# Neighbourhood attention's scores as two strided 512-column products per head, with zero-padded low parts

## The chip, the cores and the metric

One core of a Trainium2 chip runs the whole program in one launch. The metric is the time of one execution in device microseconds; a kernel's time is the median of several executions.

## What is computed

Two layers of a hybrid block work on 512 latent tokens (a grid of 8 rows by 64 columns) and 256 context tokens of width 1024. Each layer has four mixers of four heads with 64 features (neighbourhood attention, a gated linear recurrence, retention, differential attention), an output projection and a gated feed-forward. The change touches neighbourhood attention alone. For a query at grid row r and column c the keys are a window of 8 rows by 16 columns, with a relative position bias, and all 256 context tokens, under one softmax:

```python
s_win = (jnp.einsum('bqhd,brqjhd->bhqrj', qr, kw).astype(jnp.float32)
         + bias[None].astype(jnp.float32))
s_ctx = jnp.einsum('bqhd,bchd->bhqc', qr, k_ctx).astype(jnp.float32)
s = jnp.concatenate([s_win.reshape(b, h, GRID_W, n_win), s_ctx], axis=-1)
p = jax.nn.softmax(s, axis=-1).astype(v.dtype)
```

In the first layer the context's own queries also attend to the context.

## The kernel before, in words

All matrix products keep nearly full fp32 accuracy: each operand is split into a high part and the rest, its low part, and a product is made of the parts' products. For the scores the split lies along the contraction. A head has 64 features, and TensorE contracts over 128 rows, so `qk_stacks` (line 1161) builds for each head a key operand whose rows are [high; low] and a query operand whose rows are [high; high] (`stack_k`, line 985, and `stack_q`, line 996). One product over 128 rows then gives high times high plus high times low. A second product over 64 rows adds the low part of Q times the high part of K: the low parts of both heads share one tile `ql`, head 0 in rows 0 to 63 and head 1 in rows 64 to 127.

`na_unit` (line 1204) handles 128 queries of a pair of heads. Latent tokens stand in an order that makes a unit's 256 window keys a contiguous range that starts at `WBASE[j]`; the 256 context keys lie in another tile (`Kc`). So a head takes four products of 256 columns, two over 128 rows and two over 64:

```python
for ko, kk in ((0, st["K"][h][:, k]), (256, st["Kc"][h])):
    mm(o[:, ko:ko + 256], lhsT=st["Q"][h][:, q], rhs=kk, start=True, stop=False)
    mm(o[:, ko:ko + 256], lhsT=st["ql"][r, q], rhs=kk[r], start=False, stop=True)
```

VectorE then adds bias and mask and takes the maximum, ScalarE takes the exponential (`softmax_rows`, line 1244), the probabilities are turned on TensorE, copied, and multiplied with V. There are 2 layers x 2 head pairs x 4 query tiles = 16 units with 4 such pairs of products each, so 64 pairs, and `na_ctx` (line 1255) has 2 head pairs x 2 query tiles x 2 heads = 8 more, in the first layer alone. `steps_na` (line 1937) gives the units out one at a time.

The order of the instructions is not that of the code. The program is recorded, and a planner (class `Issue`, `run` at line 346) issues every instruction itself, engine by engine, from a list schedule with costs of its own: the first one of the program whose operands and places are there. Its price of a product depends on the columns alone. A string `ORDER` sets in which turn the mixers' steps enter the program, so that projections and other mixers stand between the units. Tiles are places of a few kinds: 26 of 1024 columns (T), 6 of 512 (t), 7 of 3072 (D), and in PSUM two double banks (s) and four single ones (a). The profile puts every instruction on line 535, where the planner issues it, so they are told apart by tile names and shapes: score products are `s<-T,T`.

Of the kernel before, what the change touches and what calls it, by code (L numbers as in the profile page):

```python
# [11 lines left out]
F32 = mybir.dt.float32  # L12
F32R = mybir.dt.float32r
# [73 lines left out]
class View:  # L87
    """a view of a buffer whose place is chosen later; ap: the same view of the buffer's first place"""
# [36 lines left out]
class Tag:  # L125
    """equal places for buffers"""
# [10 lines left out]
    def place(self, slot, dt):  # L137
        """of SBUF a new tile on the place, as a tile's elements keep one type"""
# [8 lines left out]
class Kind:  # L147
    """a limit on how many places buffers of a kind may hold at once, for each phase of the program"""
# [23 lines left out]
class Issue:  # L172
    """the engines' interface of a Bass: keeps the instructions, and issues them in the order of a list schedule: the
    first one of the program whose operands and places are there"""
# [25 lines left out]
    def box(self, ap, row):  # L200
        """partitions and columns (or DRAM elements) that a view touches"""
# [8 lines left out]
    def any(self, *alts):  # L210
        """one instruction that any of several engines can carry out: (engine, function, operands, options)"""
        self.add(*alts[0], alts=alts)

    @contextmanager
    def together(self):
        """TensorE's instructions that go out one right after the other"""
        self.calls = []
        yield
        calls, self.calls = self.calls, None
        self.add("tensor", "group", calls, {})  # L220
# [64 lines left out]
    def port(self, op):  # L285
        """whether it takes the SBUF port that DVE and GpSimd share: 2: its write side too"""
# [54 lines left out]
    def larger(self, b, spare, front):  # L341
        """whether a buffer can have one of the larger places"""
# [3 lines left out]
    def run(self):  # L346
# [21 lines left out]
        # a PSUM buffer is not taken before what its readers take besides it is under way  # L368
# [18 lines left out]
        def held(op, eng):  # L387
            """until when the other engine holds the port that op takes"""
# [4 lines left out]
        def start(op, now, eng):  # L393
            """the earliest time of op from now on, or None while a place has to be kept for others"""
# [22 lines left out]
        while len(order) < N:  # L417
# [50 lines left out]
            # semaphores to wait for beyond the one an instruction can carry  # L468
# [69 lines left out]
class Net:  # L538
# [35 lines left out]
    def mark(self):  # L574
        """a phase of the program begins"""
# [8 lines left out]
    def accs(self, n):  # L584
        """n times [128, 1024] in PSUM, by halves"""
# [40 lines left out]
    # ---------------------------------------------------------------- set-up  # L626
# [44 lines left out]
    def setup2(self):  # L671
# [5 lines left out]
        # softplus(y) for y = -ret_decay (broadcast), -lru_lambda (per channel)  # L677
# [28 lines left out]
        # lambda of the differential attention  # L706
# [17 lines left out]
        # relative position bias, spread over the query's column: E2[c, (l h u), X] = rpb[u, X - 1 - c]  # L724
# [13 lines left out]
    # ------------------------------------------------------------ modulation  # L738
    def mod_quarter(self, l, va, vb, q):
        """quarter q of the two vectors of a norm's shift and scale, as columns"""  # L740
# [42 lines left out]
    def mod(self, l, pairs):  # L783
        """two vectors of the modulation at a time: columns for a norm's shift and scale, or gates in DRAM"""
# [40 lines left out]
    def mod_gain(self, dst, src, o, n):  # L825
        """g_pre * (1 + scale) from columns of the scale"""
# [3 lines left out]
    def gate_rows(self, l, which, n):  # L830
        """gate * g_post on all partitions, for the latents and the context"""
# [7 lines left out]
    # ------------------------------------------------------------------ norm  # L839
    def rstd(self, ms, n):  # L840
        """(ms + eps) ** -0.5 of n columns"""
# [27 lines left out]
    def hT_alloc(self):  # L869
        """8 feature chunks of 512 latents and 256 context tokens, 4 to a tile: high and low parts"""  # L870
# [7 lines left out]
    def to_hT(self, xs, hT, part, sc, sh, pairs=range(4)):  # L878
        """xs: normed token tiles of a part -> modulated, feature-major, split"""
# [20 lines left out]
    def half_hT(self, t, late):  # L900
        """half of all token tiles, normed -> the second block's input: modulated, feature-major, split"""
# [1151 lines left out]
```

## Time and profile before

| what | value |
|---|---|
| runs | 1779.1, 1770.55, 1769.05 us (median 1770.55) |
| the profiled execution's span | 1774.8 us |
| the profiled execution's own time | 1779.1 us, the only run that is longer than the span: 4.3 us lie around it |
| PE busy | 1678.9 us (95%) |
| VectorE, ScalarE, GpSimd busy | 1251.0, 832.7, 187.9 us (70%, 47%, 11%) |
| DMA | 143 GB/s on average |

PE is TensorE's matmul side, PEld its weight loads, DVE VectorE, ACT ScalarE, POOL GpSimd. In a timeline row the first number is the start from the span's begin, the second the modelled duration. A matmul's duration contains the way through the array, so what a product costs the stream is read from one start to the next. The form `64*128 64x256` is a product over 64 rows with 128 output rows and 256 columns; `128*128 128x256` contracts over 128 rows. PEclk 1.00 is the full TensorE clock (2.4 GHz), 0.50 its lower level (1.2 GHz).

### The profile page before, as it was taken

Reading aid. Unit: us, or ns where it says so; the run is one execution under the profiler, and the core shown is the slowest. Engines: PE = TensorE matmul, PEld = TensorE weight load, DVE = VectorE, ACT = ScalarE, POOL = GpSimd, SP = SyncE. Lnnn points to the kernel's source line nnn. Section 1 sums busy time; section 2 is a strip of 40 time slices with the busy share of each in tenths; the row PEclk is TensorE's granted clock in tenths of the full one; section 3 lists DMA queues with packets and bytes.
Section 4 is the critical chain, followed back from the end, with each engine's and each line's share of the span. In section 5 each row is a group of like instructions: output and inputs, shape, how many; then the busy total and the mean of one; then the engine's idle time right before and its main releaser. Section 6 shows DMA issues by size and latency. Waiting matters only on the chain. (4 is left out here: it accounts for less than half of the span.)

```text
span 1774.8 us, 27125 instructions
## 1 busy us (share of the span) xinstructions
PE 1678.9 (95%) x10575; PEld 1446.7 (82%) x10575; DVE 1251.0 (70%) x2108; ACT 832.7 (47%) x1385; POOL 187.9 (11%) x181
## 2 busy tenths in 40 slices
PE   4899799799999999999999979999999999999997
PEld 2788677557786999999987858888877899999886
DVE  3476764654668988788679998886865688777442
ACT  3357742565656343333344466755544453343221
POOL 1010102000101101110000050132101100112000
PEclk9999999889999999999999999999997999999999
DMA  8661458744647242423665645444224443333332
GB/s 260 194 149 42 128 194 222 221 167 158 235 167 253 74 131 66 129 76 110 243 215 179 223 168 158 101 113 105 60 79 159 133 112 96 108 96 95 107 121 81
DMA packets 210456, 254.17 MB, mean 143 GB/s; under 512 B 13524, under 2 KB 163504, under 8 KB 210328
## 3 DMA queue, kind: packets, MB, share of 16 engines
q1 hardware_dynamic: 205392, 240.80, 42.8%
q0 software_dynamic: 4608, 11.54, 3.6%
q8 instruction: 83, 1.36, 0.3%
q14 instruction: 45, 0.37, 0.1%
q10 hardware_dynamic: 328, 0.11, 0.0%
HBM read 223.95 MB, written 28.69 MB: 142 GB/s over the span
## 5 line engine op out<-in xcount | busy, mean ns | idle before, releaser
L535 ACT ACT_TABLE_LOAD x41 | 52.6, 1283 | 13.0 <-PE s L535 6.9
L535 PE MATMUL s<-D_4u,D_5u 128*128 128x512 f32 (+1 forms) x66 | 18.1, 358 | 7.8 <-DVE T_3u L535 5.1
L535 PE MATMUL a<-D_0u,T_17u 128*128 128x256 f32 (+2 forms) x72 | 21.6, 331 | 0.0
L535 PE MATMUL s<-D_6u,D_4u 128*128 128x256 f32 (+1 forms) x33 | 9.9, 386 | 12.0 <-DMA D_4u<-dstk 10.7
L535 DVE TENSOR_TENSOR st_3u<-st_3u 128x1 f32<-128x1 f32 x2 | 0.3, 160 | 29.7 <-ACT T_13u L535 23.7
L535 PEld LDWEIGHTS s<-D_4u,D_5u 128*128 128x128 f32 x66 | 10.8, 190 | 11.7 <-DVE T_3u L535 5.3
L535 POOL TENSOR_TENSOR st_6u<-st_3u,mhalf_0u 128x1 f32<-128x1 f32 (+1 forms) x4 | 4.4, 1104 | 149.4 <-DVE st_3u L535 149.4
L535 ACT COPY t_3u<-s 128x384 f32<-128x384 f32 (+1 forms) x16 | 6.8, 426 | 28.5 <-PE s L535 27.9
L535 POOL DMA_DIRECT2D D_4u<-dstk x16 | 9.4, 589 | 96.1 <-DMA dstk<-T_17u 78.2
L535 PEld LDWEIGHTS s<-D_6u,D_4u 128*128 128x128 f32 x33 | 5.9, 204 | 16.5 <-issue 11.6
L535 PE MATMUL a<-D_0u,T_3u 128*128 128x256 f32 (+2 forms) x56 | 18.2, 336 | 0.0
L535 ACT ACTIVATE t_4u<-t_4u 128x384 f32<-128x384 f32 (+1 forms) x13 | 6.2, 476 | 23.6 <-DVE t_4u L535 23.6
L535 PE MATMUL a<-D_0u,T_4u 128*128 128x384 f32 (+2 forms) x60 | 16.2, 326 | 0.7 <-ACT T_1u L535 0.7
L535 PE MATMUL a<-D_0u,T_19u 128*128 128x384 f32 (+2 forms) x56 | 16.3, 339 | 0.0
L535 PE MATMUL a<-D_2u,T_1u 128*128 128x512 f32 (+1 forms) x40 | 15.2, 379 | 0.0
L535 PE MATMUL a<-D_2u,T_17u 128*128 128x512 f32 (+1 forms) x44 | 15.1, 343 | 0.0
L535 ACT COPY t_0u<-s 128x384 f32<-128x384 f32 (+1 forms) x13 | 5.8, 446 | 19.6 <-PE s L535 19.1
L535 ACT ACTIVATE t_0u<-t_0u 128x384 f32<-128x384 f32 (+1 forms) x12 | 5.9, 489 | 18.6 <-DVE t_0u L535 18.6
L535 ACT ACTIVATE T_13u<-s 128x512 f32<-128x512 f32 x4 | 2.4, 594 | 26.0 <-PE s L535 26.0
L535 PE MATMUL a<-D_3u,T_1u 128*128 128x512 f32 (+2 forms) x36 | 14.2, 394 | 0.0
L535 PE MATMUL a<-D_2u,T_3u 128*128 128x512 f32 (+1 forms) x40 | 14.1, 354 | 0.0
L535 PEld LDWEIGHTS a<-D_0u,T_17u 128*128 128x128 f32 x72 | 13.1, 190 | 1.2 <-ACT T_17u L535 0.3
(4181 smaller groups left out, 6816.8 us busy)
## 6 DMA issues: line engine op xcount, KB each, us to landing
D_4u<-dstk POOLq DMA_DIRECT2D x16, 384.0 KB, 6.9
T_6u<-in_w_mod_dram SPq DMA_DIRECT2D x8, 512.0 KB
T_20u<-in_w_mod_dram SPq DMA_DIRECT2D x7, 512.0 KB
T_4u<-in_w_mod_dram SPq DMA_DIRECT2D x7, 512.0 KB
T_21u<-in_w_in_dram SPq DMA_DIRECT2D x7, 512.0 KB
T_23u<-in_w_mod_dram SPq DMA_DIRECT2D x6, 512.0 KB
T_16u<-in_w_mod_dram SPq DMA_DIRECT2D x6, 512.0 KB
T_13u<-in_w_mod_dram SPq DMA_DIRECT2D x6, 512.0 KB
```

Source lines behind the costliest of these rows:

```text
L535: getattr(getattr(self.real, op.eng), fn)(*map(real, a), **{x: real(v) for x, v in k.items()})
```

## The change

Keys of latents and of the context now lie in one tile for each head (columns 0 to 511 and 512 to 767; the context's queries take columns 768 to 1023), so that the window and the context are two runs of 256 columns at a fixed stride, and one product reads both as its 512 columns. Each head gets its own tile half for Q's low parts, with zeros in the other 64 rows, so that the second product too contracts over all 128 rows (the rows of K's low parts meet the zeros). GpSimd writes the zeros. The context's low parts (`qlc`) are in a tile of kind t. The diff also drops comments, which is left out here.

```diff
     def stack_q(self, dst, lo, src, h, scale=None):
...
         self.scale(dst[o], src[r], s)
+        nc.gpsimd.memset(lo[o].bitcast(F32), 0.0)
         nc.vector.scalar_tensor_tensor(lo[r], src[r], s, dst[r].bitcast(F32), ALU.mult, ALU.subtract)
...
     def qk_stacks(self, l, hT, b, sq, sk, ctx):
-        K, Q = self.T(F32R, "K"), self.T(F32R, "Q")
-        KQc, ql = self.T(F32R, "KQc"), self.T(F32R, "ql")
-        st = dict(K=[K[:, 0:512], K[:, 512:1024]], Q=[Q[:, 0:512], Q[:, 512:1024]],
-                  Kc=[KQc[:, 0:256], KQc[:, 256:512]], Qc=[KQc[:, 512:768], KQc[:, 768:1024]],
-                  ql=ql[:, 0:512], qlc=ql[:, 512:768])
+        halves = lambda t: [t[:, 0:t.shape[1] // 2], t[:, t.shape[1] // 2:]]
+        ks = [self.T(F32R, "K") for _ in range(2)]
         ps, pc = self.proj(l, self.w_blk(l, sk, b), hT, True)
         for h in range(2):
-            self.stack_k(st["K"][h], ps, h)
-            self.stack_k(st["Kc"][h], pc, h)
+            self.stack_k(ks[h][:, 0:512], ps, h)
+            self.stack_k(ks[h][:, 512:768], pc, h)
         yield
+        st = dict(K=ks, Q=halves(self.T(F32R, "Q")), ql=halves(self.T(F32R, "ql")))
         ps, pc = self.proj(l, self.w_blk(l, sq, b), hT, ctx)
+        if ctx:
+            st.update(Qc=[t[:, 768:1024] for t in ks], qlc=halves(self.nc.buf("t", F32R)))
...
     def na_unit(self, l, b, st, vt, vmix, tab, out, j):
...
-                r = slice(64 * h, 64 * h + 64)
-                o = sps[:, h * 512:h * 512 + 512]
-                for ko, kk in ((0, st["K"][h][:, k]), (256, st["Kc"][h])):
-                    mm(o[:, ko:ko + 256], lhsT=st["Q"][h][:, q], rhs=kk, start=True, stop=False)
-                    mm(o[:, ko:ko + 256], lhsT=st["ql"][r, q], rhs=kk[r], start=False, stop=True)
+                o = sps[:, h * 512:h * 512 + 512].rearrange("p (a n) -> p a n", a=2)
+
+                kk = st["K"][h][:, w:1024 - w].rearrange("p (a n) -> p a n", a=2)[:, :, 0:256]
+                mm(o, lhsT=st["Q"][h][:, q], rhs=kk, start=True, stop=False)
+                mm(o, lhsT=st["ql"][h][:, q], rhs=kk, start=False, stop=True)
...
     def na_ctx(self, b, st, vt, out, j):
...
-                K = st["Kc"][h]
+                K = st["K"][h][:, 512:768]
                 o = sps[:, h * 512:h * 512 + 256]
                 mm(o, lhsT=st["Qc"][h][:, q], rhs=K, start=True, stop=False)
-                mm(o, lhsT=st["qlc"][r, q], rhs=K[r], start=False, stop=True)
+                mm(o, lhsT=st["qlc"][h][:, q], rhs=K, start=False, stop=True)
```

TensorE's order at the second unit of the first layer. T_15 holds the latents' stacked keys, T_13 those of the context, T_22 and T_12 the queries' high and low parts, so a row with 128x256 here is a score product; rows with ident are transposes for differential attention. Before:

```order
L535 MATMUL s_81<-ident_0u_102,T_5u_3299 128x128 x6
L535 MATMUL s_80<-T_15u_2993,T_22u_3289 128x256
L535 MATMUL s_80<-T_15u_2993,T_12u_3224 128x256
L535 MATMUL s_80<-T_13u_2924,T_22u_3289 128x256
L535 MATMUL s_80<-T_13u_2924,T_12u_3224 128x256
L535 MATMUL s_80<-T_15u_2993,T_22u_3289 128x256
L535 MATMUL s_80<-T_15u_2993,T_12u_3224 128x256
L535 MATMUL s_80<-T_13u_2924,T_22u_3289 128x256
L535 MATMUL s_80<-T_13u_2924,T_12u_3224 128x256
L535 MATMUL a_79<-ident_0u_102,T_6u_3353 128x128 x2
```

With the change (T_13 and T_16 are the two heads' keys, T_24 and T_3 the queries' high and low parts, the last row is a product with V in differential attention):

```order
L535 MATMUL s_81<-ident_0u_102,T_19u_3292 128x128 x6
L535 MATMUL s_80<-T_13u_2930,T_24u_3281 128x512
L535 MATMUL s_80<-T_13u_2930,T_3u_3110 128x512
L535 MATMUL s_80<-T_16u_2940,T_24u_3281 128x512
L535 MATMUL s_80<-T_16u_2940,T_3u_3110 128x512
L535 MATMUL a_78<-T_20u_3355,T_18u_865 64x128
```

The unit's eight products have become four; its neighbours are the same kinds of work. TensorE's order is unchanged up to the stretch with the first layer's units, and again from the end of the first layer's output projection to the second layer's mixers, and after these to the end. In the two stretches with units, score products, transposes, projections and the first products of the output projection change places by some rows.

GpSimd's order at the start of the program, with the change (T_7 and T_8 belong to another step, t_0 and t_1 hold the low parts of the context's queries; "x2" is both heads):

```order
L535 MEMSET T_7u_131 128x256
L535 MEMSET T_8u_133 128x256
L535 MEMSET t_0u_135 64x256 x2
L535 MEMSET t_1u_141 64x256 x2
L535 ISA
L535 TENSOR_TENSOR st_1u_228<-st_0u_213,mhalf_0u_104 128x1
```

The two rows with 64x256 are new; all others were there in this order. GpSimd's order in the first layer's mixers, with the change (T_3 and T_17 hold Q's low parts of the two head pairs, the DMA belongs to differential attention, the TENSOR_TENSOR rows are roots for norms):

```order
L535 MEMSET T_9u_2776 128x256
L535 DMA D_4u_2795<-dstk 32x4x768 x4
L535 MEMSET T_3u_3110 64x512 x2
L535 MEMSET T_17u_3573 64x512 x2
L535 TENSOR_TENSOR st_19u_3785<-st_18u_3780,mhalf_0u_104 128x12
L535 TENSOR_TENSOR st_5u_4400<-st_3u_4384,mhalf_0u_104 128x1
```

The rows with 64x512 are new, and two subtractions of 128x1024 that stood between the last two rows are gone from here: VectorE has them now. The memsets wait for nothing but a place, so the planner puts them ahead of the tiles' first use, those of the context at the very start of the program.

## Rows read from the trace of the kernel before

**Rows 1.** The page: span, busy time of the engines, granted clock in 40 slices.
```profile
span 1774.8 us, 27125 instructions
...
PE 1678.9 (95%) x10575; PEld 1446.7 (82%) x10575; DVE 1251.0 (70%) x2108; ACT 832.7 (47%) x1385; POOL 187.9 (11%) x181
...
PEclk9999999889999999999999999999997999999999
```

**Rows 2.** Timeline of PE at the first unit (start us, us, engine, line, operation, shapes, count).
```profile
367.02 0.39 PE L535 MATMUL s<-T_15u,T_22u 128*128 128x256 f32 x1
367.34 0.38 PE L535 MATMUL s<-T_15u,T_12u 64*128 64x256 f32 x1
367.65 0.38 PE L535 MATMUL s<-T_13u,T_22u 128*128 128x256 f32 x1
367.96 0.38 PE L535 MATMUL s<-T_13u,T_12u 64*128 64x256 f32 x1
```

**Rows 3.** Timeline of PE: full products that follow each other, 512 and 256 columns.
```profile
429.21 0.28 PE L535 MATMUL a<-D_1u,T_10u 128*128 128x256 f32 x1
429.33 0.28 PE L535 MATMUL a<-D_0u,T_0u 128*128 128x256 f32 x1
...
1318.36 0.40 PE L535 MATMUL a<-D_2u,T_17u 128*128 128x512 f32 x1
1318.60 0.40 PE L535 MATMUL a<-D_0u,T_17u 128*128 128x512 f32 x1
```

**Rows 4.** Timeline of PE at the half clock: units' products, then two full ones of 512 columns.
```profile
383.53 0.58 PE L535 MATMUL s<-T_15u,T_12u 64*128 64x256 f32 x1
...
384.55 0.58 PE L535 MATMUL s<-T_13u,T_12u 64*128 64x256 f32 x1
...
1342.08 0.63 PE L535 MATMUL a<-D_1u,T_1u 128*128 128x512 f32 x1
1342.51 0.63 PE L535 MATMUL a<-D_3u,T_20u 128*128 128x512 f32 x1
...
1348.48 0.58 PE L535 MATMUL s<-T_9u,T_10u 64*128 64x256 f32 x1
```

**Rows 5.** Busy time by stretch: us, busy us (instructions) by engine, PEclk, DMA share, GB/s.
```profile
core 0: us, PE busy (x) PEld busy (x) DVE busy (x) ACT busy (x) POOL busy (x), PEclk, DMA share, GB/s
366.00:381.00 15.00, 15.00 (x104) 9.26 (x106) 10.72 (x32) 9.76 (x25) 0.00 (x0) 1.00 0.48 172
381.00:392.00 11.00, 11.00 (x52) 5.91 (x46) 2.74 (x12) 4.75 (x11) 0.00 (x0) 0.54 0.71 242
...
428.00:446.00 18.00, 18.00 (x88) 12.17 (x80) 8.99 (x28) 7.98 (x18) 0.00 (x0) 1.00 0.49 165
...
1278.00:1300.00 22.00, 22.00 (x137) 15.97 (x136) 10.82 (x30) 10.76 (x23) 2.55 (x2) 1.00 0.08 25
...
1323.00:1330.00 7.00, 6.72 (x39) 5.05 (x39) 3.89 (x9) 1.56 (x2) 1.64 (x1) 0.51 0.25 75
1330.00:1333.00 3.00, 3.00 (x15) 1.93 (x13) 2.15 (x4) 2.50 (x3) 0.00 (x0) 1.00 0.80 169
1333.00:1350.00 17.00, 17.00 (x43) 11.72 (x44) 5.13 (x19) 5.20 (x11) 4.23 (x3) 0.51 0.44 157
```

**Rows 6.** Timeline of PE: the wait ahead of a unit in the second layer.
```profile
1323.28 0.58 PE L535 MATMUL s<-T_13u,T_10u 64*128 64x256 f32 x1 [2.34 <-DVE T_10u L535]
```

**Rows 7.** Timeline of POOL's memsets and of DVE beside them, and a DVE operation without.
```profile
1174.64 0.61 DVE L535 TENSOR_SCALAR T_18u<-T_18u,st_28u 128x768 f32<-128x768 f32 x1
...
1214.48 0.30 POOL L535 MEMSET T_23u<- 128x256 f32 x1
...
1215.24 0.30 POOL L535 MEMSET T_21u<- 128x256 f32 x1
...
1214.55 1.28 DVE L535 COPY T_9u<-st_7u 128x512 f32<-128x512 f32 x1 [0.54 <-POOL st_7u L535]
```

**Rows 8.** Groups of POOL's instructions: the widest memset (busy us, mean ns).
```profile
L535 POOL MEMSET T_14u<- 128x1024 f32 x1 | 1.0, 958 | 0.0
```

More of the change, by code (lines that the diff above doesn't have):

```diff
@@ L1161, in qk_stacks @@
     def qk_stacks(self, l, hT, b, sq, sk, ctx):
-        K, Q = self.T(F32R, "K"), self.T(F32R, "Q")
-        KQc, ql = self.T(F32R, "KQc"), self.T(F32R, "ql")
-        st = dict(K=[K[:, 0:512], K[:, 512:1024]], Q=[Q[:, 0:512], Q[:, 512:1024]],
-                  Kc=[KQc[:, 0:256], KQc[:, 256:512]], Qc=[KQc[:, 512:768], KQc[:, 768:1024]],
-                  ql=ql[:, 0:512], qlc=ql[:, 512:768])
+        halves = lambda t: [t[:, 0:t.shape[1] // 2], t[:, t.shape[1] // 2:]]
+        ks = [self.T(F32R, "K") for _ in range(2)]
         ps, pc = self.proj(l, self.w_blk(l, sk, b), hT, True)
         for h in range(2):
-            self.stack_k(st["K"][h], ps, h)
-            self.stack_k(st["Kc"][h], pc, h)
+            self.stack_k(ks[h][:, 0:512], ps, h)
+            self.stack_k(ks[h][:, 512:768], pc, h)
         yield
+        st = dict(K=ks, Q=halves(self.T(F32R, "Q")), ql=halves(self.T(F32R, "ql")))
         ps, pc = self.proj(l, self.w_blk(l, sq, b), hT, ctx)
+        if ctx:
+            st.update(Qc=[t[:, 768:1024] for t in ks], qlc=halves(self.nc.buf("t", F32R)))
         for h in range(2):
-            self.stack_q(st["Q"][h], st["ql"], ps, h, 0.125)
+            self.stack_q(st["Q"][h], st["ql"][h], ps, h, 0.125)
             if ctx:
-                self.stack_q(st["Qc"][h], st["qlc"], pc, h, 0.125)
+                self.stack_q(st["Qc"][h], st["qlc"][h], pc, h, 0.125)
         return st
@@ L1208, in na_unit @@
             q = slice(j * 128, j * 128 + 128)
-            k = slice(WBASE[j], WBASE[j] + 256)
+            w = WBASE[j]
             whole = lambda a: [(a, 128, 0)]
@@ L1262, in na_ctx @@
             for h in range(2):
-                r = slice(64 * h, 64 * h + 64)
-                K = st["Kc"][h]
+                K = st["K"][h][:, 512:768]
                 o = sps[:, h * 512:h * 512 + 256]
                 mm(o, lhsT=st["Qc"][h][:, q], rhs=K, start=True, stop=False)
-                mm(o, lhsT=st["qlc"][r, q], rhs=K[r], start=False, stop=True)
+                mm(o, lhsT=st["qlc"][h][:, q], rhs=K, start=False, stop=True)
             nc.vector.reduce_max(neg, sps.rearrange("p (h n) -> p h n", h=2)[:, :, 0:256], axis=AX.X, negate=True)
```

## The prediction, made before the changed kernel ran

> **What bounds the kernel now.** I read the page first, then the timeline of TensorE around the score products, then busy time by stretch. The page [rows 1] shows PE busy for 1678.9 of 1774.8 us, 95%, with DVE at 70% and the rest at half or less, and the full clock in nearly every slice. So time taken out of TensorE's stream is worth up to its full amount, if the others keep up. A busy PE need not stream, though, and the timeline shows where it does not. In a unit [rows 2] products over 128 and over 64 rows alternate, and each starts 0.31 to 0.32 us after the one before: 0.62 us from one 64-row product to the next (367.34 to 367.96). Full products that follow each other [rows 3] are 0.12 us apart at 256 columns and 0.24 us at 512. The columns of a pair are worth 0.24 us; the other 0.38 us go with the two changes between 128 and 64 rows. Nothing is waited for there: no row of rows 2 shows idle time. At the half clock [rows 4] a pair takes 1.02 us (383.53 to 384.55) and a full product of 512 columns 0.43 us (1342.08 to 1342.51).
>
> In the stretches with units PE has no gaps but one: 15.00 of 15.00 us, 18.00 of 18.00, 22.00 of 22.00 [rows 5], and one wait of 2.34 us for VectorE's write of Q's low part [rows 6]. So the gain falls on the path.
>
> **The change part by part.**
>
> *Products.* There are 64 pairs in the units and 8 in the context's attention (from the loops). Of the 64, 13 run at the half clock: 2 at 383.53 and 384.55, 3 from 1323.28, and 8 up to 1348.48 [rows 4, 6]. A pair of 256 columns, a full and a 64-row product, becomes half of a pair of 512-column products, that is one product of 512 columns in place of each pair. The new products read their columns in two runs, which no row before shows. Lower bound: 0.24 us, contiguous 512 columns [rows 3]. Upper bound: 0.62 us, if the second run were to cost as much as a change of rows [rows 2]. I take 0.24, as both runs are read by one instruction with one set of weights, and two separate 256-column products already follow each other at 2 x 0.12 [rows 3].
> - 51 pairs at the full clock: 51 x (0.62 - 0.24) = 19.4 us.
> - 13 at the half clock: 13 x (1.02 - 0.43) = 7.7 us.
> - 8 of the context: 8 x (0.62 - 2 x 0.12) = 3.0 us.
>
> Sum: 30.1 us less on PE. The zeros add no columns. Sixty-four weight loads go as well; PEld overlaps PE and is below it in every stretch [rows 5], so I count nothing for them.
>
> *Memsets.* Twelve, eight of 64x512 and four of 64x256. A memset of 256 columns takes 0.30 us [rows 7], of 1024 columns 0.96 us [rows 8], so 512 columns are about 0.52 (estimate between the two): 8 x 0.52 + 4 x 0.30 = 5.4 us on POOL, which is 11% busy. Their cover is POOL's idle time: the order puts them ahead of the tiles' first use. But they can hold DVE: a copy of 128x512 beside four memsets took 1.28 us, while a longer operation of 128x768 takes 0.61 without one [rows 7]. The Trainium skill, "SBUF — State Buffer", section "SBUF: two separate sides", says that GpSimd and some VectorE operations take turns on a shared pair of ports, and whoever comes second is blocked for the whole of the other's instruction; that speaks against writing zeros on GpSimd, the row agrees, and by it alone the twelve could cost VectorE up to 5.4 us. By the row, the context's memsets lie at the start of the program, and the eight others hold DVE for at most 4.2 us. DVE is not the path in those stretches (10.72 of 15.00 us, 8.99 of 18.00) [rows 5], so I take 1 us on the end, between 0 and 4.2.
>
> *Order.* Two weight subtractions move from POOL to DVE, and score products shift by some rows. At the changed places this is of either sign; bounds are the one wait seen in these stretches, 2.3 us [rows 6], either way per layer. I take 0.
>
> *Places.* The context's low parts hold two of six t places from the start; Q's low parts hold a T place earlier than before. The order of PE, DVE and ACT in the first stretches stays as it was, so nothing there lacks a place by the plan. Cost 0; the upper bound is once more a wait like 2.3 us [rows 6].
>
> *What is late next.* Where units follow each other closely the other engines get less time. From 366 to 381 there are 12 pairs, 12 x 0.38 = 4.6 us, which leaves 10.4 us for DVE's 10.72 and ACT's 9.76 [rows 5]. There DVE becomes the bound, and with work that cannot be packed fully I count 2 us lost. From 428 to 446 (18 pairs, 6.8 us, 11.2 left for 8.99 and 7.98) and from 1278 to 1300 (16 pairs, 6.1 us, 15.9 left for 10.82 and 10.76) they fit, but each unit's softmax sits between its scores and its transposes; 2 us for both. From 1323 to 1350 DVE and ACT are light; the 2.34 us wait stays, since the second product still needs Q's low part.
>
> Sum: 30.1 - 1 - 2 - 2 = 25 us. The profiled execution took 1779.1 us and would take 1754; it is 8.5 us above the median of the runs shown, so for the median I forecast 1770.55 - 25 = 1745.5 us.
>
> **The rivals.** Half a per cent, 9 us, is about what a measurement can tell from no change.
>
> *Softmax takes over.* VectorE and ScalarE set the pace in the stretches with units, and PE waits. For it: the stretch from 366 has no room left (above). Against: in the others DVE and ACT are at half [rows 5]. If half of the 30 us goes into waits and the memsets and subtractions cost what they can, 30 / 2 - 5 = 10 us remain: 1760.
>
> *The clock recovers.* PEclk is near a half from 381 to 392 and in two of the three stretches from 1323 to 1350 [rows 5]: about 10, 7 and 17 us, 34 in all. Less the 7.7 us already taken out, 26 us run at the half clock, which would take 13 at the full one. For it: what goes are products that leave the array without a stream for 0.38 of 0.62 us. Against: transposes and narrow products around them stay. It gives 25 + 13 = 38 us: 1732.
>
> *The clock falls for longer (slower).* Shorter products bring PE to its next wait sooner. The half clock from 1323 came right with the 2.34 us wait [rows 5, 6]. If in the stretches from 366 to 462 and 1278 to 1350 the lower clock held for longer, every microsecond of streaming done there would take two. It decides from 25 us of further work at the half clock; above 34 the kernel is slower by more than 9 us. With 45 us: 1770.5 - 25 + 45 = 1790. Against: the new products stream without a break, and PE has no idle time in nearly all of these stretches.
>
> *It does not do what it says.* If the two runs of a strided product cost 0.62 us, the upper bound, the units gain nothing and the context's 3 us are spent on memsets: 1770.
>
> **How the numbers follow.** The forecast, most of the 30 us reaching the end: 0.70, with 1735 to 1756 for its own range (all of 30 plus 5 from order; or 15). Softmax takes over: 0.13. Clock recovers: 0.10. Clock falls: 0.04. No effect: 0.03. Range: 1731 to 1760, which takes in the forecast, the recovered clock and the better half of the softmax case. Faster by over 0.5%: 0.70 + 0.10 + 0.10 of the softmax case = 0.90. Within: 0.03 + 0.03 = 0.06. Slower: 0.04.
>
> **What would show it.** In the profile after there should be no row of form 64*128 64x256 and 64 new ones of 128x512 on s; their starts 0.24 us apart at the full clock (0.62 would be the strided cost, and wrong); 64 fewer matmuls than 10575; PE's busy time down by 25 to 30 us, with its idle time up by less than 6. The stretch that was 366 to 381 should be bounded by DVE. If PE's busy time falls by 30 and the span by less than 15, the second theory is right; a longer half clock in PEclk would be the fourth. The forecast is wrong if the new products' spacing is not near 0.24, or if PE waits for DVE or ACT for more than 10 us in these stretches.

## The result, and the profile after

The changed kernel takes 1743.83 us (median of four executions, 1742.3 to 1750.7), the kernel before 1769.8 us beside it (median of four): a ratio of 0.985, 95% interval 0.981 to 0.989. That is 26 us less; 1745.5 us was forecast. A second set of six executions gives 1744.1 us and 0.987 (0.984 to 0.991).

The page of the changed kernel, answering to [rows 1] (its own execution took 1743.3 us):

```profile
span 1741.2 us, 27012 instructions
...
PE 1642.4 (94%) x10511; PEld 1425.6 (82%) x10511; DVE 1247.9 (72%) x2108; ACT 830.4 (48%) x1385; POOL 190.9 (11%) x193
...
PEclk9999899899999999999999989999999999999999
```

There are 64 matmuls and 36.5 us of PE's busy time less; DVE and ACT do what they did. PE's idle time, the span less busy, went from 95.9 to 98.8 us. The span fell by 33.6 us, more than the medians did; why is seen below.

The timeline of PE at a unit of the first layer, between products of projections, answers to [rows 2]:

```profile
422.56 0.40 PE L535 MATMUL a<-D_0u,T_0u 128*128 128x512 f32 x1
422.80 0.39 PE L535 MATMUL s<-T_1u,T_24u 128*128 128x512 f32 x1
423.03 0.39 PE L535 MATMUL s<-T_1u,T_17u 128*128 128x512 f32 x1
423.26 0.39 PE L535 MATMUL s<-T_19u,T_24u 128*128 128x512 f32 x1
423.49 0.40 PE L535 MATMUL s<-T_19u,T_17u 128*128 128x512 f32 x1
423.72 0.39 PE L535 MATMUL a<-D_0u,T_8u 128*128 128x512 f32 x1
```

The scores' products start 0.23 us apart, like the contiguous ones around them: reading the columns in two runs costs nothing. A unit takes 0.92 us (422.80 to 423.72) where an undivided unit of before took 2.4 to 2.5 from its first product to whatever follows it. The gain shrinks where products of other forms (other shapes) stand between a unit's products. In the same view, at the first layer's third unit, transposes are placed between all four:

```profile
370.32 0.50 PE L535 MATMUL s<-T_13u,T_24u 128*128 128x512 f32 x1
...
370.92 0.48 PE L535 MATMUL s<-T_13u,T_3u 128*128 128x512 f32 x1
...
371.67 0.50 PE L535 MATMUL s<-T_16u,T_24u 128*128 128x512 f32 x1
...
372.44 0.50 PE L535 MATMUL s<-T_16u,T_3u 128*128 128x512 f32 x1
```

From each of these to the next row of the timeline it takes 0.34 to 0.43 us (1.59 for the four), though all four are over 128 rows: a change to another form is paid here too.

Busy time by stretch, in the columns of [rows 5]: the units of the first layer's first head pair, and a stretch with a unit of the second layer.

```profile
362.00:378.00 16.00, 16.00 (x141) 10.21 (x137) 14.25 (x44) 13.17 (x34) 1.04 (x2) 1.00 0.54 189
...
1280.00:1300.00 20.00, 16.61 (x140) 12.71 (x140) 16.82 (x38) 12.37 (x22) 1.28 (x1) 1.00 0.42 136
```

In the first PE has no gap, and DVE is at 14.25 of 16.00 us. In the second PE is idle for 3.4 of 20.00 us, where the stretch of before with units of the same layer (1278 to 1300) had no gap at all. PE's timeline names the waits there:

```profile
1287.39 2.12 PE L535 MATMUL s<-ident_0u,T_8u 128*128 128x128 f32 x12 [1.61 <-ACT T_8u L535]
1290.67 0.43 PE L535 MATMUL s<-T_0u,T_22u 128*128 128x64 f32 x2 [1.16 <-ACT T_8u L535]
```

Transposes wait for the softmax on ScalarE, and a product behind them for ScalarE's copy of what they wrote. The wait for Q's low part [rows 6] is gone.

**What one profile cannot tell.** Each execution has a record of its mean granted clock, to three digits. The span times what is missing from 1.000 is here called the clock's share; the execution's time less that is called the rest. The share also counts lower clock in PE's waits and after its last product, where it costs nothing: 9 to 12 us of it in most of the profiles, 15 to 16 in two. So differences of it are what is read. Of 29 executions of before the clock's share has a median of 35.3 us and goes from 24.6 to 49.7, while the rest, 1731.2 us, stays within 1727.2 to 1734.5. Of the six of the changed kernel beside them the share is 31.4 us (27.8 to 36.7) and the rest 1713.0 (1711.2 to 1714.3). So the change took 18.2 us from the rest and some 4 from the clock's share, and nearly all the scatter between executions of one kernel is the clock. The profile of before that the forecast was read from was one of the unlucky ones:

```profile
core 0: 1774.8 us, clock 0.975
```

That is 44 us of clock; the changed kernel's profile has 0.982, 31 us. Counted in the stretches in which PE was busy at the half clock, half of their time is 35.4 us before and 20.1 after. So 13 to 15 us of the 33.6 between the two profiles lie in the clock. The half clock from 381, 1323 and 1333 us [rows 5] is gone after, but with such scatter one pair of profiles doesn't show that the change did it.

### The profile page after: what moved, and what is told of

Same layout as the page of the kernel before. It is cut to its first block, busy times and chain, and to the rows that moved or that the text cites. A ratio compares the mean times of both kernels' runs of the same rounds, so it can differ in the third digit from the quotient of the medians.

```text
span 1741.2 us, 27012 instructions
## 1 busy us (share of the span) xinstructions
PE 1642.4 (94%) x10511; PEld 1425.6 (82%) x10511; DVE 1247.9 (72%) x2108; ACT 830.4 (48%) x1385; POOL 190.9 (11%) x193
## 5 line engine op out<-in xcount | busy, mean ns | idle before, releaser
L535 PE MATMUL a<-D_0u,T_3u 128*128 128x256 f32 (+2 forms) x72 | 22.6, 342 | 0.0
L535 PE MATMUL s<-D_6u,D_4u 128*128 128x512 f32 (+1 forms) x32 | 9.7, 391 | 11.4 <-DMA D_4u<-dstk 10.4
L535 ACT COPY t_3u<-s 128x384 f32<-128x384 f32 (+1 forms) x16 | 6.8, 428 | 27.8 <-PE s L535 27.3
L535 PE MATMUL a<-D_0u,T_22u 128*128 128x256 f32 (+2 forms) x56 | 18.3, 339 | 0.8 <-DVE T_22u L535 0.8
L535 ACT ACTIVATE T_17u<-s 128x512 f32<-128x512 f32 x6 | 3.5, 594 | 31.3 <-PE s L535 28.3
L535 PE MATMUL a<-D_0u,T_1u 128*128 128x256 f32 (+2 forms) x56 | 18.2, 339 | 0.0
L535 ACT COPY t_2u<-s 128x384 f32<-128x384 f32 (+1 forms) x13 | 5.8, 448 | 24.0 <-PE s L535 24.0
L535 ACT ACTIVATE t_2u<-t_2u 128x384 f32<-128x384 f32 (+1 forms) x12 | 5.9, 489 | 22.8 <-DVE t_2u L535 22.8
L535 PE MATMUL a<-D_3u,T_15u 128*128 128x384 f32 (+2 forms) x52 | 16.3, 351 | 0.0
L535 PE MATMUL a<-D_2u,T_22u 128*128 128x256 f32 (+1 forms) x48 | 16.3, 339 | 0.0
L535 PE MATMUL a<-D_2u,T_15u 128*128 128x512 f32 (+1 forms) x44 | 15.6, 354 | 0.0
```

The lines of the kernel that those rows point to most:

```text
L535: getattr(getattr(self.real, op.eng), fn)(*map(real, a), **{x: real(v) for x, v in k.items()})
```

## The experiments

Each was timed beside the kernel before on the same chip, and its ratio is to that (the medians of before went from 1766 to 1772 us; the row shown is that of the call with 29 executions). "Rest" and "clock" are medians over the kernel's executions, as above; "idle" is the profile's span less PE busy; "stream" is the profile's span less idle and less half of the half-clock time in which PE was busy (before: 1774.8 - 95.9 - 35.4 = 1643.5).

| kernel | us | ratio to before (95%) | rest | clock | idle | stream |
|---|---|---|---|---|---|---|
| before | 1766.1 | 1 | 1731.2 | 35.3 | 95.9 | 1643.5 |
| the change, again | 1744.1 | 0.987 (0.984-0.991) | 1713.0 | 31.4 | 99.5 | 1622.9 |
| padded, 256 columns | 1749.6 | 0.990 (0.987-0.993) | 1714.7 | 34.9 | 104.5 | 1625.2 |
| merged, 64 rows | 1765.2 | 0.997 (0.995-1.000) | 1726.0 | 38.8 | 96.5 | 1633.2 |
| merged, 64 rows side by side | 1768.0 | 0.999 (0.997-1.002) | 1720.0 | 44.9 | 104.2 | 1625.4 |
| zeros on VectorE | 1746.4 | 0.988 (0.985-0.991) | 1714.2 | 31.4 | 102.5 | 1625.5 |
| 64 rows, the change's order | 1758.6 | 0.994 (0.992-0.997) | 1721.2 | 35.1 | 99.5 | 1630.0 |
| four together, 128 rows | 1767.1 | 0.999 (0.997-1.002) | 1724.1 | 41.5 | 114.9 | 1623.0 |
| four together, 64 rows | 1768.3 | 1.002 (0.999-1.004) | 1724.7 | 44.1 | 116.3 | 1624.6 |
| split, the change's order | 1746.5 | 0.986 (0.983-0.989) | 1712.2 | 34.0 | 96.2 | 1622.9 |
| before, full rows, no zeros | 1739.3 | 0.982 (0.979-0.984) | 1709.2 | 28.7 | 93.3 | 1621.3 |
| the same, again | 1739.6 | 0.982 (0.978-0.986) | 1710.0 | 29.5 | 94.6 | 1622.2 |
| merged, full rows, no zeros | 1750.9 | 0.989 (0.986-0.992) | 1711.7 | 40.3 | 99.6 | 1619.8 |

The first profile of the change has 98.8 us idle and a stream of 1622.4 us. Three of the expectations below (for the change's second profile, the change without zeros and the full-row kernel again) name streams that are 4 to 5 us lower, and the first of them 25 us of clock. These count the whole stretch of half clock at the program's end as PE's busy time, and PE has no product there: in the change its last one ends at 1731.3 us and that stretch begins at 1734.2. Counted as in the table they are 1622.4 for 1617.7, 1622.4 to 1622.9 for 1617.8, 1621.3 for 1617.5, and 20.1 for the 25 us.

The theories: (1) the gain is the changes between products over 128 and over 64 rows; (2) it is having fewer, longer products; (3) 64-row products bring on the half clock; (4) the planner's new order makes or takes some of it.

### Padding without merging

```diff
-                o = sps[:, h * 512:h * 512 + 512].rearrange("p (a n) -> p a n", a=2)
-                kk = st["K"][h][:, w:1024 - w].rearrange("p (a n) -> p a n", a=2)[:, :, 0:256]
-                mm(o, lhsT=st["Q"][h][:, q], rhs=kk, start=True, stop=False)
-                mm(o, lhsT=st["ql"][h][:, q], rhs=kk, start=False, stop=True)
+                o = sps[:, h * 512:h * 512 + 512]
+                for ko, kk in ((0, st["K"][h][:, w:w + 256]), (256, st["K"][h][:, 512:768])):
+                    mm(o[:, ko:ko + 256], lhsT=st["Q"][h][:, q], rhs=kk, start=True, stop=False)
+                    mm(o[:, ko:ko + 256], lhsT=st["ql"][h][:, q], rhs=kk, start=False, stop=True)
```

> The changed kernel with the low parts padded to 128 rows as in the change, but each head's scores again as four products of 256 columns, window and context apart. Theory 1 (the gain is the two changes of rows that leave each pair, 0.38 us): the products stand 0.12 us apart at the full clock as in rows 3, a unit of eight takes about 0.95 us as the changed kernel's four take (0.92), and the time is within 6 us of the changed kernel's 1743.8. Theory 2 (the gain comes from fewer, longer products and fewer weight loads): a pair stays nearer 0.62 us than 0.24 and the time is at 1760 or above, near the 1769.8 of before.

1749.6 us. PE's timeline of this kernel, half of a unit of eight products:

```profile
427.20 0.28 PE L535 MATMUL s<-T_7u,T_24u 128*128 128x256 f32 x1
427.32 0.28 PE L535 MATMUL s<-T_7u,T_20u 128*128 128x256 f32 x1
427.44 0.28 PE L535 MATMUL s<-T_7u,T_24u 128*128 128x256 f32 x1
427.56 0.28 PE L535 MATMUL s<-T_7u,T_20u 128*128 128x256 f32 x1
```

0.12 us each, against 0.31 in [rows 2]: padding alone removes the cost. Whether the 5.8 us to the change are the missing merge or the other order of the planner was left to the run that splits in the change's own order.

### Merging without padding

```diff
-        nc.gpsimd.memset(lo[o].bitcast(F32), 0.0)
...
-                mm(o, lhsT=st["ql"][h][:, q], rhs=kk, start=False, stop=True)
+                r = slice(64 * h, 64 * h + 64)
+                mm(o, lhsT=st["ql"][h][r, q], rhs=kk[r], start=False, stop=True)
...
```

> The changed kernel's strided products of 512 columns, but the low parts over the 64 rows of their head, without zeros (the context's too). Theory 1: one pair of 512 columns has two changes left where before two pairs had four, so it takes 0.24 + 0.24 + 0.38 = 0.86 us, a unit 1.7 us where it took 2.5 before and takes 0.92 after; of the 64 + 8 pairs' changes 32 go, 32 x 0.38 = 12 us off PE at the full clock, and the time is about 1758. Theory 2: a pair takes about 0.5 us and the time is the changed kernel's 1744 or a little less, as the memsets are gone.

1765.2 us: not theory 2, and 7 us above what theory 1 gave. PE's timeline of this kernel, from the first product of a unit to the one behind it:

```profile
367.23 0.40 PE L535 MATMUL s<-T_13u,T_24u 128*128 128x512 f32 x1
367.56 0.49 PE L535 MATMUL s<-T_13u,T_19u 64*128 64x512 f32 x1
367.98 0.50 PE L535 MATMUL s<-T_16u,T_24u 128*128 128x512 f32 x1
368.41 0.49 PE L535 MATMUL s<-T_16u,T_19u 64*128 64x512 f32 x1
368.83 0.32 PE L535 MATMUL a<-T_1u,T_18u 128*64 128x128 f32 x1
```

A product behind a change takes 0.42 to 0.43 us where 0.23 are its columns: 0.19 to 0.20 a change, so 0.85 for a pair, as expected; only the change behind this unit's first product costs less, 0.10 (367.23 to 367.56). The stream is 10.3 us longer than that of the change's second profile (12 expected). The rest is 13 us longer and the clock's share 7 us larger. What part of these is the order and what the rows, this kernel does not show, as its order is its own.

### Both heads' 64-row products side by side

No zeros, as in the kernel just above, and a unit's four products issued right behind each other.

```diff
...
+            with nc.together():
+                for lo in range(2):
+                    for h in range(2):
+                        r = slice(64 * h, 64 * h + 64) if lo else slice(0, 128)
...
+                        mm(o, lhsT=st["ql" if lo else "Q"][h][r, q], rhs=kk[r], start=not lo, stop=bool(lo))
```

> As the kernel with strided 512-column products and 64-row low parts, but a unit's four products are issued one right behind the other: both heads' 128-row products, then both heads' 64-row products, which lie in different halves of the rows. Theory 1 with a price per change: two changes are left in a unit, so it takes 4 x 0.24 + 0.38 = 1.33 us, 0.4 us more than the changed kernel's 0.92, 16 x 0.4 = 6.6 us in all, and the time is about 1750 less what the memsets cost (0 to 4 us). Rival: the two 64-row products, being in different halves, run beside each other and take 0.24 us together; then a unit takes about 1.1 us and the time is 1744 or below. Second rival: going from one half of the rows to the other is a change too, 0.19 us more: 1.5 us a unit, 1753.

PE's timeline of this kernel, from the first product of a unit:

```profile
367.86 0.40 PE L535 MATMUL s<-T_13u,T_24u 128*128 128x512 f32 x1
368.10 0.40 PE L535 MATMUL s<-T_16u,T_24u 128*128 128x512 f32 x1
368.43 0.50 PE L535 MATMUL s<-T_13u,T_19u 64*128 64x512 f32 x1
368.43 0.50 PE L535 MATMUL s<-T_16u,T_19u 64*128 64x512 f32 x1
368.86 0.32 PE L535 MATMUL a<-T_1u,T_18u 128*64 128x128 f32 x1
```

The first rival holds for the products: the two of 64 rows start together, and a unit takes 1.00 us, 0.08 more than with zeros. The Trainium skill, "TensorE: Matmul & The Clock Gate", "Part 3: Packing small matmuls — row/col tiling", says that products in different groups of rows run at the same time; the rows agree. Yet the kernel takes 1768.0 us, 24 more than the change. The 16 units' products can't be the cause: 16 x 0.08 = 1.3 us. Its rest is 7 us longer than the change's and its clock's share 13.5 us larger.

### Zeros on VectorE

```diff
-        nc.gpsimd.memset(lo[o].bitcast(F32), 0.0)
+        nc.vector.memset(lo[o].bitcast(F32), 0.0)
```

> The changed kernel with the twelve memsets on VectorE instead of GpSimd, where they take VectorE's own time. If the memsets cost the end what was counted for them (1 us, at most 4.2), the time moves by less than 5 us either way from the changed kernel's 1743.8: 5.4 us more busy time on VectorE in all, which is 72% busy. If VectorE is what sets the pace in the stretches with units, as counted for the one from 366 to 381, the four of the first layer that fall near it add up to 2 us to the time there. Anything beyond 5 us would come from the planner's other order, not from the zeros.

1746.4 us (1744.4 to 1752.2) against 1744: the zeros are not worth anything that can be seen, on either engine. In the changed kernel the two rows of zeros for a head pair took 1.10 us together (0.52 each were estimated). The timeline of POOL and DVE there:

```profile
375.69 1.10 POOL L535 MEMSET T_17u<- 64x512 f32 x2 [36.84 <-PE a L535]
...
375.77 0.47 DVE L535 TENSOR_SCALAR st_6u<-st_4u 128x2 f32<-128x2 f32 x1
...
378.68 0.17 DVE L535 TENSOR_SCALAR st_7u<-st_5u 128x2 f32<-128x2 f32 x1
```

An operation on two columns took 0.47 us beside the zeros and 0.17 without, so 0.3 us more; the copy in [rows 7] was longer beside memsets too.

### 64 rows, with every instruction in the change's place

The planner prices a product by its columns, so reading 64 of the 128 rows leaves the order of every engine as it is; the zeros are still written and no longer read.

```diff
-                mm(o, lhsT=st["ql"][h][:, q], rhs=kk, start=False, stop=True)
+                r = slice(64 * h, 64 * h + 64)
+                mm(o, lhsT=st["ql"][h][r, q], rhs=kk[r], start=False, stop=True)
```

> The changed kernel with every instruction in its place, zeros too, but the second product of each head of a unit reads only the 64 rows that are not zeros. The order of all engines is that of the changed kernel, so nothing but the change of rows differs. Theory 1 (a price of 0.38 us per pair of changes): 32 x 0.38 = 12 us more stream, and the time is 1744 + 12 = 1756. Theory 3 (the 64-row products also bring on the half clock): more than that, 1762 or above, with the half clock near the units. If the order alone made the kernels with 64-row products slow (1765 and 1768), the time is 1744 to 1750.

1758.6 us, 14.5 more than the change in the same call, where theory 1 gave 12. PE's timeline of this kernel at the unit that starts at 420.81 in the change, between projections of 256 columns:

```profile
430.92 0.28 PE L535 MATMUL a<-D_2u,T_0u 128*128 128x256 f32 x1
431.04 0.39 PE L535 MATMUL s<-T_1u,T_24u 128*128 128x512 f32 x1
431.36 0.50 PE L535 MATMUL s<-T_1u,T_17u 64*128 64x512 f32 x1
431.79 0.50 PE L535 MATMUL s<-T_19u,T_24u 128*128 128x512 f32 x1
432.22 0.49 PE L535 MATMUL s<-T_19u,T_17u 64*128 64x512 f32 x1
432.64 0.39 PE L535 MATMUL a<-D_2u,T_8u 128*128 128x256 f32 x1
```

1.60 us from first to next against 0.92, with the same instructions around. The rest is 8.2 us longer (1721.2 against 1713.0), the idle time is the same 99.5 us: order and waits have no part in it. This is the cleanest evidence for theory 1: half of the changes of rows, put back alone, cost 7 us of stream and 8 us of rest. It is less than 12, because this unit's first change costs 0.09 (431.04 to 431.36 is 0.32) and not 0.19, and because products that stand beside transposes pay a change either way. The clock's share is 35.1 us against 31.4, but goes from 29.7 to 51.3, so theory 3 is neither shown nor excluded, and the part of the 14.5 us beyond the rest is not shown to be the rows'. In this profile the half clock stands beside units again:

```profile
379.00:389.00 10.00, 10.00 (x44) 4.77 (x44) 2.96 (x14) 4.18 (x9) 1.04 (x2) 0.51 0.54 176
1297.00:1307.00 10.00, 8.80 (x44) 6.70 (x45) 7.30 (x15) 6.22 (x11) 0.00 (x0) 0.52 0.21 76
```

### The change, a second profile

> The changed kernel itself once more, for a second profile. Split each profile's span into PE's idle time, the time given up while PE was busy at the half clock (half of it), and the rest, the stream. If the 14 us of clock that the change's first profile shows beyond before are the change's own, the half clock stands at the same places again and takes 25 us, within 3. If they are chance, it stands elsewhere and the sum differs by 5 us or more; the stream, 1617.7 us, should agree within 3 us either way.

Idle 99.5 and stream 1622.9 us repeat the first profile (98.8, 1622.4), and the clock took 19.3 us of PE's busy time against 20.1. So the sum held, but not all the places: this profile has half clock from 1287.0 us for 6.8 us, where the first has the full clock (1.00 from 1280 to 1300, above). Busy time by stretch and PE's waits there, in the second profile:

```profile
1280.00:1300.00 20.00, 16.82 (x127) 13.17 (x126) 16.61 (x37) 12.11 (x22) 1.28 (x1) 0.83 0.38 124
1285.49 2.51 PE L535 MATMUL s<-ident_0u,T_8u 128*128 128x128 f32 x12 [1.62 <-ACT T_8u L535]
1289.16 0.69 PE L535 MATMUL s<-T_0u,T_22u 128*128 128x64 f32 x2 [1.16 <-ACT T_8u L535]
```

The waits there are those of the first profile (1.61 and 1.16 us), in the same order of instructions. Where the lower clock falls is partly the execution's.

### Four together, over 128 rows and over 64

A unit's four products are issued right behind each other, high parts first. In one kernel the low products read 128 rows with zeros, in the other 64; the second's order is the first's, instruction by instruction.

```diff
+            with nc.together():
+                for lo in range(2):
+                    for h in range(2):
...
+                        mm(o, lhsT=st["ql" if lo else "Q"][h][r, q], rhs=kk[r], start=not lo, stop=bool(lo))
```

> The changed kernel with a unit's four products issued right behind each other: both heads' high parts, then both heads' low parts, all over 128 rows with zeros. It costs no change of rows, so a unit takes 0.92 us and what differs from 1744 is the planner's order alone: within 6 us either way if its order is of no matter, up to 15 more if it is as large a term as the gain itself.

> As the kernel with four products together over 128 rows, every instruction in the same place, but the two low products read only the 64 rows of their head and so can run beside each other. Its order is that of its twin over 128 rows. By the spacings seen with the other order a unit takes 1.00 us against 0.92: 16 x 0.08 = 1.3 us more, no difference that can be measured. If the pair of 64-row products brings on the half clock, or costs a change going in and one going out with nothing won, it is 6 us or more slower than its twin.

1767.1 and 1768.3 us. The twins differ by 1.2 us, in the stream by 1.6 (1.3 expected): 64-row products side by side really cost next to nothing more than padded ones. And the twin with the same products as the change is 23 us slower than the change. Between their profiles lie 24 us: the streams are equal within 0.1 us, PE is idle for 114.9 us instead of 99.5, and half clock takes 27.9 us of its busy time instead of 19.3. PE's timeline of the kernel over 128 rows has a wait of 10.8 us, where the change waits 5.3 at most behind 470 us, and others that the change lacks:

```profile
1051.93 0.90 PE L535 MATMUL s<-ident_0u,T_11u 128*128 128x128 f32 x3 [10.81 <-ACT T_11u L535]
...
1289.13 1.97 PE L535 MATMUL s<-ident_0u,T_11u 128*128 128x128 f32 x8 [3.49 <-DVE T_11u L535]
1292.51 0.45 PE L535 MATMUL s<-ident_0u,T_8u 128*128 128x128 f32 x1 [1.41 <-DVE T_11u L535]
```

Busy time by stretch of the same kernel, at the second and third of these waits and at two more of 1.7 us and 1.1 us:

```profile
1284.00:1296.00 12.00, 6.64 (x33) 4.66 (x34) 6.71 (x18) 5.36 (x12) 1.64 (x1) 0.59 0.00 1
...
1400.00:1412.00 12.00, 8.83 (x51) 7.21 (x49) 9.37 (x15) 8.33 (x13) 2.06 (x3) 0.73 0.85 222
```

Around these waits the granted clock is 0.59 and 0.73. That the waits bring the lower clock is not shown: around the like waits of the change it was 1.00 in one profile and 0.83 in the other. This is theory 4: the planner's order, changed by asking that four products stay together, is worth as much as the whole change. It is also what is left to explain the slow kernel with side-by-side products, whose own order was not tested apart: the twins show that such products do not cost it.

### Splitting in the change's order

Where the planner issues a head's second product, four products of 256 columns are issued for the two of 512. At three of the 32 heads the planner had put other heads' products in between; there the four take another head's high part, which alters the output and not the number or shape of the products.

```diff
...
+                elif n == 0:
+                    high = k
+                else:
+                    for i in range(2):
+                        for kk in (high, k):
+                            self.real.tensor.matmul(real(a[0])[:, i], **{**kk, "rhs": kk["rhs"][:, i]})
...
```

> The changed kernel with its order kept on every engine, but where the planner issues a head's second product, four padded products of 256 columns over 128 rows are issued in place of the two of 512. Only merging is undone. Theory 1 (the gain is the changes of rows, merging is worth nothing by itself): 8 x 0.12 = 0.96 us a unit against 0.92, so under 1 us more in all and the time is within 3 us of 1744. Theory 2 (fewer, longer products are worth something): the 5.8 us by which the padded kernel with 256 columns and its own order was slower come back, 1750.

1746.5 us (1738.7 to 1754.5), 0.986 against the change's 0.985 and 0.987; the rest is 1712.2 against 1713.0 and the stream the same 1622.9 us. Theory 2 falls: merging by itself is worth nothing that can be seen, and the 5.8 us of the first experiment are left to its order (its idle time is 5 us longer).

### Before with full rows, no zeros

The low parts of both heads already fill one tile, so the product can simply read all its rows. What it adds is the other head's low part of Q times this head's low part of K, as small a term as the one the split leaves out.

```diff
-                    mm(o[:, ko:ko + 256], lhsT=st["ql"][r, q], rhs=kk[r], start=False, stop=True)
+                    mm(o[:, ko:ko + 256], lhsT=st["ql"][:, q], rhs=kk, start=False, stop=True)
...
-                mm(o, lhsT=st["qlc"][r, q], rhs=K[r], start=False, stop=True)
+                mm(o, lhsT=st["qlc"][:, q], rhs=K, start=False, stop=True)
```

> The kernel before with one edit: the low products read all 128 rows of the shared tile ql (and of the context's), with no zeros, no new tiles and no merging. The other head's rows then add the product of its Q's low part with this head's K's low part, a term as small as what the split leaves out anyway. Its order is nearer to that of before than the change's is. Theory 1: all changes of rows are gone, 64 x 0.38 + 3.0 = 27 us less stream, and the time is 1766 - 27 = 1739, up to 10 more if its order costs waits. Theory 2: within 6 us of before, 1760 to 1770.

1739.3 us, where 1739 was expected. PE's timeline of this kernel, the start of a unit:

```profile
423.14 0.28 PE L535 MATMUL s<-T_18u,T_3u 128*128 128x256 f32 x1
423.26 0.28 PE L535 MATMUL s<-T_18u,T_5u 128*128 128x256 f32 x1
423.38 0.28 PE L535 MATMUL s<-T_7u,T_3u 128*128 128x256 f32 x1
423.50 0.29 PE L535 MATMUL s<-T_7u,T_5u 128*128 128x256 f32 x1
```

T_5u holds the low parts of both heads. Two lines, no zeros, no new tiles, no merging, and the kernel gains all that the change gains and some more: a stream of 1621.3 us, 1 to 2 below the change's, and 5 to 6 us less idle time.

> The kernel before with the low products over all 128 rows of the shared tile, once more. If the 1739.3 us and the ratio 0.9816 hold, it is 5 us faster than the change (1743.8 and 1744.1, ratios 0.9848 and 0.9873): expected is 1736 to 1743 with a ratio below 0.985. If the first result was a lucky set of executions, the median is 1744 or above. In the profile the stream should be 1617.5 within 1 us, with the clock's share anywhere from 17 to 30 us.

1739.6 us, ratio 0.982 again. Against the change's 1743.8 and 1744.1 it is 4 to 5 us ahead, twice. The intervals of the ratios still overlap a little (0.978 to 0.986 and 0.984 to 0.991), so that it is the fastest of all is likely, not certain.

### The change without zeros

```diff
-        nc.gpsimd.memset(lo[o].bitcast(F32), 0.0)
...
-        st = dict(K=ks, Q=halves(self.T(F32R, "Q")), ql=halves(self.T(F32R, "ql")))
+        ql = self.T(F32R, "ql")
+        st = dict(K=ks, Q=halves(self.T(F32R, "Q")), ql=[ql[:, 0:512]] * 2)
...
-            st.update(Qc=[t[:, 768:1024] for t in ks], qlc=halves(self.nc.buf("t", F32R)))
+            st.update(Qc=[t[:, 768:1024] for t in ks], qlc=[ql[:, 512:768]] * 2)
```

> The changed kernel with both heads' low parts in one tile again, read over all 128 rows, without zeros (the same small extra term as above): two strided products of 512 columns a head, no memsets, a tile less for each head pair. Theory 1: the products cost what the change's do, 0.92 us a unit, so it differs from the change by the zeros (no more than 1 us, by the run with zeros on VectorE) and by the planner's order, which can be worth up to 20 us, as in the kernels with four products together: 1740 to 1764, with a stream within 4 us of 1617.8.

1750.9 us. The stream is the shortest of all, 1619.8 us, and the rest and the idle time are the change's (1711.7 against 1713.0, 99.6 against 99.5); the 7 us lie in the clock's share, 40.3 us. So the lower clock can last longer without 64-row products and without more idle time in all; why it does here stays open.

## Why the prediction held, step by step

*What bounds it, and why a pair costs 0.62 us.* Right. The price of the changes between 128 and 64 rows was read off the start times of [rows 2, 3], and putting half of them back with nothing else moved cost 7 us of stream and 8 us of rest. Filling the rows alone, in the kernel before, gave the whole gain.

*The new product's 0.24 us.* Right: 0.23, and the two runs of columns are free.

*The sum of 30.1 us less on PE.* About right for the profile that it was read from, too high for the median. Counted from each score product's start to the next product's, waits left out, the 144 products of before (72 pairs) take 48.2 us in that profile and the 80 in their place (64, and 16 of the context) 19.3: 28.9 less. But at the full clock the pairs come to 27.4 us of stream (72 x 0.38), and the stream fell by 21.1 us. An undivided unit saves 1.4 to 1.5 us, where 4 x 0.38 = 1.52 was counted. A unit with transposes between its products keeps its changes of form: 1.59 us left where 0.92 was counted. That each of the 72 pairs loses both changes was the assumption that failed. The 2.8 us that the 13 half-clock pairs added came from a single execution; the clock's share fell by about 4 us between the medians. PE's busy time fell by 36.5 us, more than the 25 to 30 named as a sign, since 15 of it are clock.

*Memsets, 1 us.* Nothing could be seen, within the bounds.

*DVE becomes the bound from 366 to 381, 2 us.* Wrong: PE has no gap there, with DVE at 14.25 of 16.00 us. *Softmax between, 2 us.* The place was right, the size too small: 3.4 us of idle time at 1280 to 1300, where before had none. *The 2.34 us wait stays.* Wrong, it went. Together PE's idle time grew by 2.9 us, where 4 were counted.

*Order, 0 us between 2.3 either way per layer.* No run reads the value apart from the waits above; the bounds are too narrow for what an order can do. The same products in another order of the planner cost 23 us, five times the 4.6 us of both layers, as 15 us of waits and 9 us of clock in the profile. With such a draw the change would have been no gain at all, and the prediction, which had given 9 in 10 to a gain, had no rival for it.

So the 22 us between the medians of the second set are 21 us of stream, less 3 of new waits, plus some 4 of clock, where 25 were forecast. That 1743.8 us came within 2 us of the forecast is luck: errors of a few microseconds cancelled. "The clock recovers" looked right in the pair of profiles (no half clock is left in the places it named), but the executions show that most of that was the one profile. "The clock falls for longer" did not come: 20.1 us of PE's busy time against 35.4. "It does not do what it says" is excluded by the spacings. "Softmax takes over" is excluded for this order (PE's idle time grew by 2.9 us, not 15).

## What to carry to other kernels

Read what a product costs from start to start, and look for places where products over 128 and fewer rows alternate: filling the rows, with zeros or simply with what is already in them, can be cheaper than the smaller product, and two half-height products in different halves of the rows are nearly as good if they stand together (1.2 us between the twins). When a list schedule sets the order, test what an edit does to the products with the order held fixed; the schedule's own reaction can be as large as the effect. Split each execution into the clock's share and the rest before reading a gain out of two profiles.

## What the runs showed of the hardware that was not expected

- A change of rows costs 0.19 to 0.20 us in each direction where such products alternate, at 256 columns (0.31 - 0.12) and at 512 (0.43 - 0.23) alike: it is a price per change, not per column. Behind a run of projections over 128 rows a unit's first change costs half of that (0.32 - 0.23); why stays open.
- Two 64-row products in different halves start at the same instant (368.43 and 368.43) and together with the change behind them take 0.43 us, where a single one with its change takes 0.42 (367.56 to 367.98).
- Nearly all the scatter between executions is the granted clock: over 29 executions of before the clock's share spans 25 us and the rest 7 us.
- The lower clock does not follow waits or rows alone: with 15 us more idle time 9 us more of PE's busy time went to it in one kernel, but the change without zeros gave up 9 us more than the change with the same idle time, and the same waits of the change had 1.00 around them in one execution and 0.83 in another.
